# Hybrid decoder trunk on one NeuronCore: the triangular inverse of the recurrent stage on 16x16 blocks

## The chip, the cores and the metric

The kernel runs on one core of a Trainium2 chip. The metric is the device time of one execution in microseconds (us). A core has a matrix engine (TensorE, PE in the profile; its weight loads are listed apart as PEld), a vector engine (VectorE, DVE), a scalar engine (ScalarE, ACT), a general engine (GpSimd, POOL) and a queue that issues transfers (SyncE, SP). Each engine runs its own instructions in order and waits for others by semaphores. Products land in PSUM, which is read by DVE and ACT; the rest lives in SBUF.

## What is computed

One layer: RMSNorm, one input projection of 1024 x 4224 on 2048 tokens, and three branches side by side, each with a SiLU gate: differential attention (4 heads), a short gated convolution, and RWKV-7 time mixing (4 heads of size 64). The gated branches are joined, projected (1024 x 1024), added to the input and normalised. The RWKV branch is a recurrence over tokens:

```python
def step(state, inp):
    r_t, k_t, v_t, w_t, kk_t, a_t = inp
    sa = jnp.einsum('bhvk,bhk->bhv', state, kk_t)
    state = (state * w_t[:, :, None, :]
             - sa[..., None] * (kk_t * a_t)[:, :, None, :]
             + v_t[..., None] * k_t[:, :, None, :])
    y = jnp.einsum('bhvk,bhk->bhv', state, r_t)
    return state, y
```

Taken in chunks of 64 tokens, the feedback through `sa` inside a chunk becomes a unit triangular system of 64 x 64, and its inverse (Z in the code) turns the chunk into matrix products; only one 64 x 64 state per head goes from chunk to chunk.

## The kernel before

The tokens are worked in two halves of 1024. After a start stage (loads, norm, the projections that the recurrence needs) come four stages in this order: the recurrence of half 0 (called rwkv0 here), the attention of half 0, the recurrence of half 1 (rwkv1), the attention of half 1; a tail ends the output projection.

**Order on TensorE.** TensorE's order is that of the program text, written out by hand: each stage is a Python generator that yields hints (an amount of time), and `run` fills each hint with matmuls from one long list, the filler (`filler`): projections still to be made, and at the end the 16 tiles of the output projection (`out_tile`, L1184, 48 matmuls each). A hint f in a stage with factor `scale` draws matmuls of `T512` = 0.216 hint units each until f x scale is used up. SCALE is 0.6 for rwkv0 and 0.55 for rwkv1, 1.0 for attention. The other engines' orders are the compiler's. Output tile i is held back while i >= `allowed`; that is 8 until the first block of head 3 in the last attention is finished, and then 10, 12, 14, 16.

**The recurrent stage** (`rwkv`, L455) has 8 units per half, one for each 256 tokens and two heads. A unit passes through `early` (loads, decay, norms), `scores` (L549: scores G of the chunk, masked into N, BB and DE; part of N is written to memory as `ud` and read back as U in a layout with blocks spread over partitions), `inverse` (L632) and `late` (L660). The units are staggered: while `late` of unit n is emitted, after each of its yields one step of `early` and `scores` of unit n+2 follows, and then `inverse` of unit n+2.

**`inverse`** inverts the 32 x 32 diagonal blocks by substitution on DVE: 16 steps, each a multiplication (`tmpx`, L646) and a sum (`Xs`, L649) over 128 partitions. The result goes through memory (`zd`) into the diagonal blocks of Z.

**`late`** puts 64 x 64 inverses together: transposes of Z on TensorE (`xp`, L673), a copy to X, a product with N (`p4`, L680), a scaled copy into P1, a second product (`p5`, L685), an addition into Z (L688). All are 128 x 128 matmuls on block diagonal matrices. Then `wu` (Z times AB, L696), the products M and RW (`mr`, L717, L718) in two groups, and the short chain over the chunks (`chp`, `yp`, L738, L743) in which each step waits for a DVE copy of the state (`Ss`, L740).

PSUM has four pools here; `ps_w` (two buffers, `pw`) holds p4 and p5 together in one tile, and lw, la, ssp, bc2, vap, bvp, yp, vpp and bcp2; `ps_s` (three buffers, `pS`) holds G, tp, xp, wu, mr and the attention's scores.

**Broadcasts.** A factor per token is spread over 128 columns by a matmul with the identity: `bcp` (L538, L765), `obc` (L1066, 32 pairs in the attention stages) and `hbc` (`spread`, L251).

Of the kernel before, what the change touches and what calls it, by code (L numbers as in the profile page):

```python
# [24 lines left out]
NJ = 2  # L25
# [62 lines left out]
def _table(cols):  # L88
    t, o = {}, 0
    for n, w in cols:  # L90
# [7 lines left out]
                      ("eye", 32 * GW), ("hmean", 2), ("id64", 64), ("mB", 2)))  # L98
# [4 lines left out]
def host_consts():  # L103
    c, cr = np.zeros((P, NCON), np.float32), np.zeros((P, NCONR), np.float32)

    def put(n, a):
        d, (o, w) = (c, CON[n]) if n in CON else (cr, CONR[n])
        d[:, o:o + w] = a

    p = np.arange(P)  # L110
    t = np.arange(64)
    put("ident", np.eye(P))
    put("le", (p[:, None] % 64) <= t[None])
    put("lt", (p[:, None] % 64) < t[None])
# [5 lines left out]
    eye = np.eye(32).reshape(32, NG, GW).transpose(1, 0, 2).reshape(NG, 1, 32 * GW)  # L120
    put("eye", np.tile(eye.reshape(NG, 32 * GW), (NB, 1)))
# [24 lines left out]
def trunk(ctx, tc, a, o, phases="RTO"):  # L146
# [308 lines left out]
    def rwkv(half, pool):  # L455
# [21 lines left out]
        P1 = pool.tile([P, NQ, P], F32, name="P1")  # L477
        nc.gpsimd.memset(P1, 0.0)
        mB = C("mB")
# [7 lines left out]
        def early(s, n, g, ct):  # L487
# [61 lines left out]
        def scores(s):  # L549
# [17 lines left out]
            for jj in range(NJ // 2):  # L567
                for h in range(2):
                    G = pS("G")
                    for q in range(4):  # L570
                        j, e = jj * 2 + q // 2, q % 2
                        mm(G[:, q * P:(q + 1) * P], KB[h * 64:h * 64 + 64, j, 2 * e:2 * e + 2],  # L572
                           RA[h * 64:h * 64 + 64, :, j, 1 - e], start=True, stop=True)
                    Gv = G.rearrange("p (j e m t) -> p j e m t", j=2, e=2, m=2)
                    q0 = h * NJ + jj * 2
                    for e in range(2):
                        nr = slice(64 * e, 64 * e + 64)
                        sr = slice(64 - 64 * e, 128 - 64 * e)
                        lt = C("lt").unsqueeze(1).broadcast_to([P, 2, 64])
                        tt(N[sr, q0:q0 + 2, sr], Gv[sr, :, e, 1], lt[sr], ALU.mult)  # L580
# [5 lines left out]
            U = T("U", (P, 32, 32), bufs=2)  # L586
            ud = dr.tile([NB, 32, 32], F32, name="ud", bufs=2)
            for e in range(2):
                for b in range(2):
                    q0 = (e * 2 + b) * NQ  # L590
                    r0 = 64 - 64 * e + b * 32
                    dma(ud[q0:q0 + NQ].rearrange("q s t -> s q t"), N[r0:r0 + 32, :, r0:r0 + 32])
# [39 lines left out]
        def inverse(s):  # L632
            U, Z = s["U"], s["Z"]


            pr = T("U2", (P, 32, 16))
            Uf = U.rearrange("p s t -> p (s t)")
            tt(pr, U[:, :, 0:32:2], Uf[:, 1:1024:66].unsqueeze(1).broadcast_to([P, 32, 16]), ALU.mult)
            tt(U[:, :, 1:32:2], U[:, :, 1:32:2], pr, ALU.add)
            nc.gpsimd.memset(Uf[:, 0:1024:33], 1.0)  # L640
            Xs = T("Xs", (P, 32, GW))
            cpy(Xs, C("eye").rearrange("p (a b) -> p a b", a=32))
# [7 lines left out]
            Zs = T("Zs", (P, GW, 32))  # L650
            cpy(Zs, Xs.rearrange("p a b -> p b a"))
            zd = dr.tile([NB, 32, 32], F32, name="zd", bufs=2)
            dma(zd.rearrange("b (g c) i -> (b g) c i", c=GW), Zs)
            for e in range(2):
                for b in range(2):
                    q0 = (e * 2 + b) * NQ
                    r0 = 64 - 64 * e + b * 32
                    dma(Z[r0:r0 + 32, :, r0:r0 + 32], zd[q0:q0 + NQ].rearrange("q c i -> c q i"))

        def late(s):  # L660
            ct, gc, o0, N, Z = (s[n] for n in ("ct", "gc", "o0", "N", "Z"))
# [3 lines left out]
            Z2 = Z.rearrange("p q (b n) -> p q b n", b=2)  # L665
            Pb2 = P1.rearrange("p q (b n) -> p q b n", b=2)
# [3 lines left out]
            X = T("X", (P, NQ, 64))  # L670
            xp = pS("xp")
            for q in range(NQ):
                nc.tensor.transpose(xp[:, q * P:(q + 1) * P], Z[:, q], ident)  # L673
            yield LQ[0]
            cpy(X.rearrange("p q (b n) -> p (q b) n", b=2), xp.rearrange("p (q n) -> p q n", n=64)[:, :, 0:32])
            yield LQ[0]
            p45 = pw("p45")
            p4, p5 = p45[:, 0:NQ * 64], p45[:, NQ * 64:2 * NQ * 64]
            for q in range(NQ):
                mm(p4[:, q * 64:(q + 1) * 64], N[:, q], X[:, q], start=True, stop=True)  # L680
            yield LQ[0]
            act(Pb2[:, :, :, 0:32], p4.rearrange("p (q b n) -> p q b n", q=NQ, b=2), AF.Copy, scale=mB[:, 0:1])
            yield LQ[0]
            for q in range(NQ):
                mm(p5[:, q * 64:(q + 1) * 64], P1[:, q], Z2[:, q, :, 32:64], start=True, stop=True)  # L685
            yield LQ[0]
            Z64 = Z.rearrange("p q (b n) -> p (q b) n", b=2)
            stt(Z64[:, :, 32:64], p5.rearrange("p (q n) -> p q n", n=32), mB[:, 1:2], Z64[:, :, 32:64], ALU.mult,  # L688
                ALU.add)
# [13 lines left out]
            for r0 in (0, 64):  # L703
                nc.gpsimd.memset(Z[r0:r0 + 32, :, r0 + 32:r0 + 64], 0.0)
# [4 lines left out]
            RW = T("RW", (P, NJ, 2, 64))  # L709
            for e in range(2):  # L710
                sr = slice(64 - 64 * e, 128 - 64 * e)
                mr = pS("mr")[:, 0:2 * WR // 2]
                for h in range(2):
                    hs = slice(h * 64, h * 64 + 64)
                    for j in range(NJ):
                        q = h * NJ + j
                        mm(mr[hs, j * 64:j * 64 + 64], W[sr, q], KBm[sr, j * 2 + e, hs], start=True, stop=True)  # L717
                        mm(mr[hs, (NJ + j) * 64:(NJ + j) * 64 + 64], W[sr, q], DE[sr, q, e], start=True, stop=True)  # L718
                yield LQ[1]
                mr4 = mr.rearrange("p (m j n) -> p m j n", m=2, j=NJ)  # L720
# [43 lines left out]
            for j in range(NJ):  # L764
                mm(bcp[:, j * P:(j + 1) * P], rvb[:, 2 * j:2 * j + 2].rearrange("p a b -> p (a b)"), ident,  # L765
                   start=True, stop=True)
# [77 lines left out]
    def attention(half, nlam, bt, pool, after=None):  # L844
# [207 lines left out]
        def finish(h, pr, ob, sq, zs):  # L1052
# [12 lines left out]
            for j in range(2):  # L1065
                mm(bc[:, j * P:(j + 1) * P], rp[:, j:j + 1].broadcast_to([P, P]), ident, start=True, stop=True)  # L1066
# [318 lines left out]
```

## Time and profile before

| what | value |
|---|---|
| runs | median 1798.87 us of three (1794.3 to 1798.88) |
| the profiled execution | 1790.98 us, of which the span from first to last instruction is 1789.2 us |
| TensorE busy | 1615.6 us (90%) |
| DVE, POOL, ACT busy | 1229.6, 822.4, 733.4 us |
| mean granted TensorE clock | 0.955 of full speed |

Busy time counts overlapping matmuls once. Where the clock column says 0.50, TensorE had the lower of its two clocks (1.2 instead of 2.4 GHz). Waits are put down to the instruction that released them.

### The profile page before, as it was taken

What the parts mean: (1) busy time and instruction counts of PE and PEld (TensorE: products, weight loads), DVE (VectorE), ACT (ScalarE), POOL (GpSimd) and SP (SyncE); (2) the same over time, 40 slices, a digit from 0 to 9 for tenths busy, and PEclk for the clock granted to TensorE, in tenths of its full rate; (3) what the DMA queues carried; (4) which work ended last, traced back from release to release, by engine and by line L of the source; (5) the groups of instructions that cost most, each with busy time, mean ns of one, the idle gap of its engine ahead of it and who ended that gap; (6) DMA issues with size and microseconds to landing.
All of it is one profiled execution on the core that took longest, in us unless ns stands there. A gap on an engine that the chain in (4) does not pass through costs nothing.

```text
span 1789.2 us, 27288 instructions
## 1 busy us (share of the span) xinstructions
PE 1615.6 (90%) x9416; PEld 1300.2 (73%) x9416; DVE 1229.6 (69%) x2653; ACT 733.4 (41%) x1797; POOL 822.4 (46%) x794
## 2 busy tenths in 40 slices
PE   5899799999999878999799989998988979999998
PEld 4687576776788766778576767786777868877786
DVE  7633866677516788874766776518899898888842
ACT  5331111122115655552121222125656667767742
POOL 6433232333157886444132322275377375363243
PEclk9899898899899989999898999999999989999999
DMA  5343222222245634224222222253234243222223
GB/s 188 100 141 97 67 67 58 81 78 60 64 136 177 210 117 124 77 68 132 89 86 58 87 72 67 72 171 96 70 98 129 76 148 114 87 90 78 90 88 112
DMA packets 136586, 179.86 MB, mean 101 GB/s; under 512 B 34912, under 2 KB 83072, under 8 KB 136448
## 3 DMA queue, kind: packets, MB, share of 16 engines
q1 hardware_dynamic: 136448, 178.13, 31.9%
q8 instruction: 74, 1.21, 0.3%
q14 instruction: 64, 0.52, 0.1%
HBM read 131.92 MB, written 46.14 MB: 100 GB/s over the span
## 4 chain that ended last, share of the span: by engine, by line
PE 48%; DVE 33%; DMA 5%; issue 4%; ACT 4%; SPq 3%; POOL 3%; DVEq 0%; POOLq 0%; ACTq 0%
PE pj L343 23%; PE ops L1200 7%; DVE tmpx L646 5%; DVE P L992 4%; DVE Xs L649 3%; PE aT L1027 3%; DVE nm L949 3%; PE G L572 2%; SPq L594 2%; PE S L943 2%; PE S L944 2%; PE av L1020 2%; PE av L1018 1%; PE av L1019 1%; DVE x L242 1%
## 5 line engine op out<-in xcount | busy, mean ns | idle before, releaser
L343 PE MATMUL pj<-hh,wh 128*128 128x512 f32 x1008 | 420.7, 417 | 8.5 <-DVE raw L394 4.7
L343 PE MATMUL pj<-hl,wh 128*128 128x512 f32 x1008 | 420.5, 417 | 0.0
L343 PE MATMUL pj<-hh,wl 128*128 128x512 f32 x1008 | 419.9, 417 | 0.0
L952 ACT ACTIVATE P<-S,nm 128x512 f32<-128x512 f32 (+3 forms) x320 | 199.3, 624 | 151.1 <-DVE nm L949 134.9
L343 PEld LDWEIGHTS pj<-hh,wh 128*128 128x128 f32 x1008 | 195.7, 194 | 48.2 <-ACT hh L245 5.1
L329 POOL TENSOR_TENSOR wl<-wr,wh 128x1024 fp32r<-128x1024 f32 x85 | 209.2, 2461 | 46.0 <-ACT wh L324 41.0
L949 DVE TENSOR_REDUCE nm<-S 128x1 f32<-128x512 f32 (+3 forms) x320 | 191.5, 604 | 50.9 <-PE S L944 47.6
L343 PEld LDWEIGHTS pj<-hl,wh 128*128 128x128 f32 x1008 | 195.7, 194 | 40.0 <-issue 3.0
L343 PEld LDWEIGHTS pj<-hh,wl 128*128 128x128 f32 x1008 | 195.2, 194 | 40.3 <-issue 2.8
L992 DVE SCALAR_TENSOR_TENSOR P<-P,sc 128x512 f32<-128x512 f32 (+3 forms) x160 | 148.0, 950 | 6.8 <-ACT P L976 4.6
L326 POOL TENSOR_SCALAR wh<-wr 128x1024 fp32r<-128x1024 f32 x70 | 76.8, 1098 | 148.7 <-PE pj L343 142.2
L943 PE MATMUL S<-K,QH 128*128 128x512 f32 (+2 forms) x320 | 124.8, 390 | 22.2 <-ACT P L952 21.9
L646 DVE TENSOR_TENSOR tmpx<-U,Xs 128x16 f32<-128x16 f32 (+15 forms) x256 | 130.9, 511 | 6.6 <-POOL U L640 1.2
L1027 PE MATMUL aT<-con,P 128*128 128x128 f32 x576 | 91.6, 283 | 35.9 <-DVE aTl L1034 25.8
L944 PE MATMUL S<-K,QL 128*128 128x512 f32 (+2 forms) x320 | 119.0, 372 | 0.0
L1034 DVE TENSOR_TENSOR aTl<-aT,aTh 128x512 fp32r<-128x512 f32 x144 | 98.3, 684 | 26.5 <-ACT aTh L1033 24.9
L1027 PEld LDWEIGHTS aT<-con,P 128*128 128x128 f32 x576 | 70.0, 144 | 58.2 <-DVE aTl L1034 29.9
L1033 ACT CAST aTh<-aT 128x512 fp32r<-128x512 f32 x144 | 83.5, 583 | 51.3 <-PE aT L1027 50.7
L1200 PE MATMUL ops<-woh,wl 128*128 128x512 f32 x256 | 102.1, 399 | 0.0
L1200 PE MATMUL ops<-woh,wh 128*128 128x512 f32 x256 | 102.1, 399 | 0.0
L1200 PE MATMUL ops<-wol,wh 128*128 128x512 f32 x256 | 102.1, 399 | 0.0
L948 DVE TENSOR_TENSOR S<-S,bt 128x256 f32<-128x256 f32 (+1 forms) x152 | 57.2, 377 | 62.7 <-PE S L944 61.6
(337 smaller groups left out, 3345.4 us busy)
## 6 DMA issues: line engine op xcount, KB each, us to landing
wr<-in_wt_dram SPq DMA_DIRECT2D x85, 512.0 KB, 3.7
rawk<-pk SPq DMA_DIRECT2D x96, 128.0 KB, 2.8
U<-ud SPq DMA_DIRECT2D x128, 64.0 KB, 2.3
rawq<-pq SPq DMA_DIRECT2D x128, 64.0 KB, 2.3
wr<-mx SPq DMA_DIRECT2D x128, 64.0 KB, 2.0
oxt<-in_x_dram SPq DMA_DIRECT2D x32, 256.0 KB, 3.0
out_dram<-oxt SPq DMA_DIRECT2D x32, 256.0 KB, 2.1
prw<-s SPq DMA_DIRECT2D x28, 256.0 KB, 2.1
```

The lines of the kernel that those rows point to most:

```text
L329: nc.gpsimd.tensor_tensor(wl[:, ks], wr[:, ks], wh[:, ks].bitcast(F32), ALU.subtract)
L343: mm(ps, lhs[:, k], rhs[c][k], start=(n == 0), stop=(n == 3 * NK - 1))
L646: tt(tmp[:, :, :, 0:m], U[:, 0:m, i:i + 2].rearrange("p j r -> p r j").unsqueeze(2).broadcast_to([P, 2, GW, m]), Xs[:, 0:m].rearrange("p j ...
L943: mm(s[:, 0:sw], QH[:, m, off:off + P], K[:, m, 0:sw], start=True, stop=False)
L944: mm(s[:, 0:sw], QL[:, m, off:off + P], K[:, m, 0:sw], start=False, stop=True)
L949: nc.vector.tensor_reduce(nm[:, m, g:g + 1], s[:, 0:gw], AX.X, ALU.max, negate=True)
L952: act(p[:, 0:gw], s[:, 0:gw], AF.Exp, bias=nm[:, m, g:g + 1], accum_out=l[:, m, g:g + 1])
L992: stt(p1, p1, sc[:, 1, g:g + 1], p0, ALU.mult, ALU.add)
L1027: nc.tensor.transpose(t[:, d * 256 + qi * P:d * 256 + qi * P + P], x["A"][g][:, ko:ko + P], ident)
L1033: cpy(th, t)
L1034: tt(tl, t, th.bitcast(F32), ALU.subtract)
L1200: mm(ps, l[:, k], Ws[n][r][k], start=(c == 0), stop=(c == 3 * NK - 1))
```

## The change

Substitution works on 16 x 16 blocks: 8 steps in place of 16, with at most 128 in place of 256 products a partition in one. U, `ud` and `zd` shrink with it; the transfers of one unit become 8 writes of `ud` (4 before), 4 reads of U (8 before), 1 write of `zd`, and 8 reads into Z0 (4 before). 32 x 32 inverses are then made from 16 x 16 ones, and 64 x 64 from 32 x 32, each by two sets of small products on 32 x 32 tiles of the array; X comes from 32 x 32 transposes on DVE; N and Z hold only the 64 columns that are used. `late` has three more yields of `LQ[0]` = 0.9, and one yield of 2 x 0.5 where there were two of 0.5. `wu` is made of 64 x 64 tiles. The G products of both heads, and the `mr` products of both row halves, are issued alternately into two PSUM tiles. The broadcasts become transposes.

```diff
-NB = 4 * NQ
+BL = 16
+NB = 128 // BL * NQ
 NG = 128 // NB
-GW = 32 // NG
+GW = BL // NG
...
     def spread(rs, ps=None):
...
-            mm(ps[:, j * P:(j + 1) * P], rs[:, j:j + 1].broadcast_to([P, P]), ident, start=True, stop=True)
+            nc.tensor.transpose(ps[:, j * P:(j + 1) * P], rs[:, j:j + 1].broadcast_to([P, P]), ident)
...
-            for n, w in (("N", P), ("Z", P)):
+            for n, w in (("N", 64), ("Z", 64), ("Z0", 32)):
                 m[n] = pool.tile([P, NQ, w], F32, name=f"{n}{i}")
+            for n in ("Z", "Z0"):
                 nc.gpsimd.memset(m[n], 0.0)
...
             for j in range(NJ):
-                mm(bcp[:, j * P:(j + 1) * P], rnb[:, 2 * j:2 * j + 2].rearrange("p a b -> p (a b)"), ident,
-                   start=True, stop=True)
+                nc.tensor.transpose(bcp[:, j * P:(j + 1) * P], rnb[:, 2 * j:2 * j + 2].rearrange("p a b -> p (a b)"),
+                                    ident)
...
             for jj in range(NJ // 2):
+                Gs = [pS("G") for _ in range(2)]
+                for q in range(4):
+                    j, e = jj * 2 + q // 2, q % 2
+                    for h in range(2):
+                        mm(Gs[h][:, q * P:(q + 1) * P], KB[h * 64:h * 64 + 64, j, 2 * e:2 * e + 2],
+                           RA[h * 64:h * 64 + 64, :, j, 1 - e], start=True, stop=True)
                 for h in range(2):
-                    G = pS("G")
-                    for q in range(4):
-                        j, e = jj * 2 + q // 2, q % 2
-                        mm(G[:, q * P:(q + 1) * P], KB[h * 64:h * 64 + 64, j, 2 * e:2 * e + 2],
-                           RA[h * 64:h * 64 + 64, :, j, 1 - e], start=True, stop=True)
+                    G = Gs[h]
...
+            for r0 in (*range(64, 128, BL), *range(0, 64, BL)):
+                c0, q0 = r0 % 64, r0 // BL * NQ
+                dma(ud[q0:q0 + NQ].rearrange("q s t -> s q t"), N[r0:r0 + BL, :, c0:c0 + BL])
...
-            for i in range(0, 32, 2):
-                tmp = T("tmpx", (P, 2, GW, 32), bufs=1)
+            for i in range(0, BL, 2):
+                tmp = T("tmpx", (P, 2, GW, BL), bufs=1)
...
+            for r0 in range(0, P, BL):
+                c0, q0 = r0 % 32, r0 // BL * NQ
+                dma(Z0[r0:r0 + BL, :, c0:c0 + BL], zd[q0:q0 + NQ].rearrange("q c i -> c q i"))
...
+            X = T("X", (P, NQ, 32), bufs=2)
+            nc.vector.transpose(X, Z0)
             p45 = pw("p45")
+            p4, p5 = p45[:, 0:NQ * 16], p45[:, NQ * 16:NQ * 48]
+            blocks = [slice(r0, r0 + 32) for r0 in range(0, P, 32)]
             yield LQ[0]
             for q in range(NQ):
+                for rs in blocks:
+                    c0 = rs.start % 64
+                    mm(p4[rs, q * 16:(q + 1) * 16], N[rs, q, c0:c0 + 32], X[rs, q, 0:16], start=True, stop=True)
             yield LQ[0]
+            stt(P0[:, :, 0:16], p4.rearrange("p (q n) -> p q n", n=16), C("hi16"),
+                C("id16").unsqueeze(1).broadcast_to([P, NQ, 16]), ALU.mult, ALU.add)
+            yield LQ[0]
+            for q in range(NQ):
+                for rs in blocks:
+                    mm(p5[rs, q * 32:(q + 1) * 32], P0[rs, q], Z0[rs, q], start=True, stop=True)
+            yield LQ[0]
+            for i, rs in enumerate(blocks):
+                c0 = rs.start % 64
+                (nc.vector.tensor_copy if i % 2 == 0 else cpy)(Z[rs, :, c0:c0 + 32],
+                                                               p5[rs].rearrange("p (q n) -> p q n", n=32))
+
+            X = T("X", (P, NQ, 32), bufs=2)
+            for rs in blocks[0::2]:
+                nc.vector.transpose(X[rs], Z[rs, :, 0:32])
+            P1 = T("P1", (P, NQ, 32))
+            p45 = pw("p45")
+            p4, p5 = p45[:, 0:NQ * 32], p45[:, NQ * 32:2 * NQ * 32]
+            yield LQ[0]
+            for q in range(NQ):
+                for r0 in (0, 64):
+                    up, lo = slice(r0, r0 + 32), slice(r0 + 32, r0 + 64)
+                    mm(p4[lo, q * 32:(q + 1) * 32], N[up, q, 32:64], X[up, q], start=True, stop=True)
+            yield LQ[0]
+            cpy(P1[32:64], p4[32:64].rearrange("p (q n) -> p q n", n=32))
+            nc.vector.tensor_copy(P1[96:128], p4[96:128].rearrange("p (q n) -> p q n", n=32))
+            yield LQ[0]
+            for q in range(NQ):
+                for r0 in (0, 64):
+                    up, lo = slice(r0, r0 + 32), slice(r0 + 32, r0 + 64)
+                    mm(p5[up, q * 32:(q + 1) * 32], P1[lo, q], Z[lo, q, 32:64], start=True, stop=True)
+            yield LQ[0]
+            cpy(Z[0:32, :, 32:64], p5[0:32].rearrange("p (q n) -> p q n", n=32))
+            nc.vector.tensor_copy(Z[64:96, :, 32:64], p5[64:96].rearrange("p (q n) -> p q n", n=32))
             yield LQ[0]
...
-                    mm(wu[:, (h * NJ + j) * P:(h * NJ + j + 1) * P], Z[:, h * NJ + j], AB[:, j, h], start=True, stop=True)
+                    for hs in (slice(0, 64), slice(64, 128)):
+                        mm(wu[hs, (h * NJ + j) * P:(h * NJ + j + 1) * P], Z[hs, h * NJ + j], AB[hs, j, h], start=True,
+                           stop=True)
...
+            mrs = [pS("mr")[:, 0:2 * WR // 2] for _ in range(2)]
+            for j in range(NJ):
+                for what in range(2):
+                    for h in range(2):
+                        hs, q = slice(h * 64, h * 64 + 64), h * NJ + j
+                        for e in range(2):
+                            sr = slice(64 - 64 * e, 128 - 64 * e)
+                            mm(mrs[e][hs, (what * NJ + j) * 64:(what * NJ + j) * 64 + 64], W[sr, q],
+                               DE[sr, q, e] if what else KBm[sr, j * 2 + e, hs], start=True, stop=True)
+            yield 2 * LQ[1]
...
-                mm(bc[:, j * P:(j + 1) * P], rp[:, j:j + 1].broadcast_to([P, P]), ident, start=True, stop=True)
+                nc.tensor.transpose(bc[:, j * P:(j + 1) * P], rp[:, j:j + 1].broadcast_to([P, P]), ident)
```

## Rows read from the trace of the kernel before

**Rows 1.** The profile page: busy us, share of the span, instructions.
```profile
PE 1615.6 (90%) x9416; PEld 1300.2 (73%) x9416; DVE 1229.6 (69%) x2653; ACT 733.4 (41%) x1797; POOL 822.4 (46%) x794
```
**Rows 2.** Busy time by window: PE, PEld, DVE, ACT, POOL, clock, DMA share, GB/s.
```profile
160.00:511.00 351.00, 321.68 (x2215) 247.96 (x2214) 232.66 (x607) 67.22 (x170) 108.20 (x119) 0.93 0.22 66
...
822.00:1169.00 347.00, 316.98 (x2230) 243.95 (x2229) 224.09 (x604) 74.26 (x184) 105.70 (x123) 0.95 0.27 83
```
**Rows 3.** TensorE's waits in 160 to 511: total us, times, longest.
```profile
PE chp L738 <- DVE Ss L740: 9.8, 6, 3.8
PE xp L673 <- DMA Z<-zd: 8.6, 1, 8.6
```
**Rows 4.** TensorE's waits in 822 to 1169.
```profile
PE xp L673 <- DMA Z<-zd: 7.1, 2, 5.4
PE chp L738 <- DVE Ss L740: 4.5, 4, 2.7
```
**Rows 5.** Timeline of all engines, 440.5 to 446.2: start, duration, instruction.
```profile
441.22 0.66 DVE L646 TENSOR_TENSOR tmpx<-U,Xs 128x256 f32<-128x256 f32 x1
...
442.32 2.49 POOL L329 TENSOR_TENSOR wl<-wr,wh 128x1024 fp32r<-128x1024 f32 x1
...
442.52 2.44 DVE L558 TENSOR_TENSOR RA<-in_r,PL 128x128 f32<-128x128 f32 x1
...
445.56 0.48 PE L738 MATMUL chp<-Ss,M 64*64 64x64 f32 x4 [2.43 <-DVE Ss L740]
```
**Rows 6.** Busy time by window, 450 to 455, columns as in rows 2.
```profile
450.00:455.00 5.00, 5.00 (x26) 3.48 (x24) 2.29 (x9) 0.56 (x2) 0.00 (x0) 0.50 0.04 7
```
**Rows 7.** DVE's groups by line: busy us, mean ns, idle before.
```profile
L646 DVE TENSOR_TENSOR tmpx<-U,Xs 128x16 f32<-128x16 f32 (+15 forms) x256 | 130.9, 511 | 6.6 <-POOL U L640 1.2
L649 DVE TENSOR_REDUCE Xs<-tmpx 128x8 f32<-128x16 f32 (+15 forms) x256 | 74.8, 292 | 6.0
```
**Rows 8.** TensorE's timeline, one unit: blocks of matmuls and what starts next.
```profile
405.12 1.16 PE L572 MATMUL G<-RA,KB 64*128 64x128 f32 x8
406.20 0.50 PE L343 MATMUL pj<-hh,wl 128*128 128x512 f32 x1
...
415.14 0.68 PE L618 MATMUL bvp<-VU,BB 64*64 64x64 f32 x16
415.75 0.50 PE L343 MATMUL pj<-hh,wl 128*128 128x512 f32 x1
...
418.16 0.61 PE L765 MATMUL bcp<-con,sqy 128*128 128x128 f32 x4
418.52 0.48 PE L343 MATMUL pj<-hl,wh 128*128 128x512 f32 x1
...
426.22 1.00 PE L680 MATMUL p<-X,N 128*128 128x64 f32 x8
427.03 0.48 PE L343 MATMUL pj<-hh,wl 128*128 128x512 f32 x1
...
437.55 0.32 PE L717 MATMUL mr<-KBm,W 64*64 64x64 f32 x2
...
438.44 0.50 PE L343 MATMUL pj<-hh,wh 128*128 128x512 f32 x1
```
**Rows 9.** Timeline, ACT's groups, and waits of weight loads around lw.
```profile
423.34 0.70 PE L496 MATMUL lw<-in_thw,wup 64*128 64x256 f32 x2
...
L501 ACT ACTIVATE e<-lw,der 128x256 f32<-128x256 f32 x16 | 7.6, 476 | 32.4 <-PE la L498 23.3 <-PE lw L496 9.2
...
PEld p L680 <- ACT e L501: 3.5, 9, 0.4
```
**Rows 10.** Chain in order of time; output matmuls until 1643; a window before it.
```profile
89.24 65.76 PE pj L343 x281
...
L1200 PE MATMUL ops<-woh,wh x120: 387/393/628, 1444.7 to 1642.8; 128*128 128x512 f32 x120
...
1600.00:1643.00 43.00, 41.30 (x230) 34.95 (x229) 34.97 (x75) 30.71 (x76) 19.18 (x21) 1.00 0.23 73
```

More of the change, by code (lines that the diff above doesn't have):

```diff
@@ L119, in host_consts @@
     put("cmat", np.eye(P) - same / 64.0)
-    eye = np.eye(32).reshape(32, NG, GW).transpose(1, 0, 2).reshape(NG, 1, 32 * GW)
-    put("eye", np.tile(eye.reshape(NG, 32 * GW), (NB, 1)))
+    eye = np.eye(BL).reshape(BL, NG, GW).transpose(1, 0, 2).reshape(NG, BL * GW)
+    put("eye", np.tile(eye, (NB, 1)))
+    put("hi16", (p[:, None] % 32) >= 16)
+    put("id16", (p[:, None] % 32) == np.arange(16)[None])
+    put("id16b", (p[:, None] % 32) == 16 + np.arange(16)[None])
     put("hmean", ((p[:, None] // 64) == np.arange(2)[None]) / 64.0)
@@ L472, in rwkv @@
             m = {}
-            for n, w in (("N", P), ("Z", P)):
+            for n, w in (("N", 64), ("Z", 64), ("Z0", 32)):
                 m[n] = pool.tile([P, NQ, w], F32, name=f"{n}{i}")
+            for n in ("Z", "Z0"):
                 nc.gpsimd.memset(m[n], 0.0)
             mats.append(m)
-        P1 = pool.tile([P, NQ, P], F32, name="P1")
-        nc.gpsimd.memset(P1, 0.0)
-        mB = C("mB")
+        P0 = pool.tile([P, NQ, 32], F32, name="P0")
+        nc.gpsimd.tensor_copy(P0[:, :, 16:32], C("id16b").unsqueeze(1).broadcast_to([P, NQ, 16]))
         def T(n, shape=(P, WR), bufs=1):
@@ L585, in scores @@
                        C("le").unsqueeze(1).broadcast_to([P, 4, 64]), ALU.mult)
[L586 to L592, printed above, removed]
+            U = T("U", (P, BL, BL), bufs=2)
+            ud = dr.tile([NB, BL, BL], F32, name="ud", bufs=2)
+            for r0 in (*range(64, 128, BL), *range(0, 64, BL)):
+                c0, q0 = r0 % 64, r0 // BL * NQ
+                dma(ud[q0:q0 + NQ].rearrange("q s t -> s q t"), N[r0:r0 + BL, :, c0:c0 + BL])
             for cg in range(NG):
@@ L632, in inverse @@
         def inverse(s):
[L633 to L636 removed]
+            U, Z0 = s["U"], s["Z0"]
+            h2 = BL // 2
+            pr = T("U2", (P, BL, h2))
             Uf = U.rearrange("p s t -> p (s t)")
[L638 to L642, printed above, removed]
[L643 to L644 removed]
+            tt(pr, U[:, :, 0:BL:2], Uf[:, 1:BL * BL:2 * BL + 2].unsqueeze(1).broadcast_to([P, BL, h2]), ALU.mult)
+            tt(U[:, :, 1:BL:2], U[:, :, 1:BL:2], pr, ALU.add)
+            nc.gpsimd.memset(Uf[:, 0:BL * BL:BL + 1], 1.0)
+            Xs = T("Xs", (P, BL, GW))
+            cpy(Xs, C("eye").rearrange("p (a b) -> p a b", a=BL))
+            for i in range(0, BL, 2):
+                tmp = T("tmpx", (P, 2, GW, BL), bufs=1)
                 m = i + 2
@@ L649, in inverse @@
                 nc.vector.tensor_reduce(Xs[:, i:i + 2], tmp[:, :, :, 0:m], AX.X, ALU.add)
-            Zs = T("Zs", (P, GW, 32))
+            Zs = T("Zs", (P, GW, BL))
             cpy(Zs, Xs.rearrange("p a b -> p b a"))
-            zd = dr.tile([NB, 32, 32], F32, name="zd", bufs=2)
+            zd = dr.tile([NB, BL, BL], F32, name="zd", bufs=2)
             dma(zd.rearrange("b (g c) i -> (b g) c i", c=GW), Zs)
[L654 to L658, printed above, removed]
+            for r0 in range(0, P, BL):
+                c0, q0 = r0 % 32, r0 // BL * NQ
+                dma(Z0[r0:r0 + BL, :, c0:c0 + BL], zd[q0:q0 + NQ].rearrange("q c i -> c q i"))
         def late(s):
-            ct, gc, o0, N, Z = (s[n] for n in ("ct", "gc", "o0", "N", "Z"))
+            ct, gc, o0, N, Z, Z0 = (s[n] for n in ("ct", "gc", "o0", "N", "Z", "Z0"))
             RA, DE, VU, VU4, AB, KBm = (s[n] for n in ("RA", "DE", "VU", "VU4", "AB", "KBm"))
@@ L669, in late @@
                                     s["PC"].unsqueeze(2).broadcast_to([P, NC, 64]), ALU.mult)
[L670 to L676, printed above, removed]
-            p45 = pw("p45")
-            p4, p5 = p45[:, 0:NQ * 64], p45[:, NQ * 64:2 * NQ * 64]
@@ L679, in late @@
[L679 to L682, printed above, removed]
+            X = T("X", (P, NQ, 32), bufs=2)
+            nc.vector.transpose(X, Z0)
+            p45 = pw("p45")
+            p4, p5 = p45[:, 0:NQ * 16], p45[:, NQ * 16:NQ * 48]
+            blocks = [slice(r0, r0 + 32) for r0 in range(0, P, 32)]
@@ L709, in late @@
             RW = T("RW", (P, NJ, 2, 64))
-            for e in range(2):
[L711 to L720, printed above, removed]
+            mrs = [pS("mr")[:, 0:2 * WR // 2] for _ in range(2)]
[8 more added lines that the diff above has]
+            yield 2 * LQ[1]
+            for e in range(2):
+                mr4 = mrs[e].rearrange("p (m j n) -> p m j n", m=2, j=NJ)
                 tt(M[:, :, e], mr4[:, 0], dP4[:, :, e], ALU.add)
@@ L764, in late @@
             for j in range(NJ):
-                mm(bcp[:, j * P:(j + 1) * P], rvb[:, 2 * j:2 * j + 2].rearrange("p a b -> p (a b)"), ident,
-                   start=True, stop=True)
+                nc.tensor.transpose(bcp[:, j * P:(j + 1) * P], rvb[:, 2 * j:2 * j + 2].rearrange("p a b -> p (a b)"),
+                                    ident)
             yield LQ[1]
```

14 lines of the change are left out of this document (2 added, 12 removed).

## The prediction

> **What bounds the kernel now.** I read the page first: TensorE is busy 90% of the span [rows 1], so what a change wins must come out of TensorE's idle time, its clock or its own work, and what it adds there it loses. Then the windows by stage, since the change lives in two stages. In rwkv0 (160 to 511) TensorE is busy 321.7 of 351 us, in rwkv1 (822 to 1169) 317.0 of 347 [rows 2]: 29.3 + 30.0 = 59 us idle. The clock column is the second loss: 0.93 and 0.95, so 0.07 x 351 + 0.05 x 347 = 42 us of full-speed work is missing. DVE is busy only two thirds of these stages, but that is an average.
>
> Then the waits of TensorE in these stages. Two kinds stand out: the first `late` of each half waits for Z from the inverse, 8.6 + 7.1 us, and the chain over the chunks waits for DVE's copy of the state, 9.8 + 4.5 us in ten places [rows 3, 4]. The timeline shows why the copy is late [rows 5]: at 441 DVE still runs the last substitution steps of another unit (0.66 us for one multiplication) between the short operations that `late` needs, one of those is stretched to 2.44 us while POOL runs a 2.49 us subtraction, and the chunk product at 445.56 has waited 2.43 us. The wait has an echo: at 450 to 455 TensorE is busy all the time, at clock 0.50, the lower of its two levels [rows 6], and it had idled just before. So a stall of 2 us costs more than 2 us. Shorter substitution can take both away.
>
> **The substitution.** One unit spends (130.9 + 74.8) / 16 = 12.9 us of DVE in the 16 steps [rows 7]. The 8 steps that stay have the shapes of the smaller half (up to 128 products a partition); at 0.7 of the mean durations that is 8 x 0.7 x (0.51 + 0.29) = 4.5 us, an estimate. Work that comes to DVE: three transposes, one small fused operation and four copies out of PSUM. No row shows a DVE transpose; it lies between nothing and, as an estimate, the 0.3 us of a reduction in the steps removed [rows 7], which is what I take, for eight operations 2.4 us less one that goes. DVE is relieved by 12.9 - 4.5 - 2 = about 6 us a unit, and the inverse of a unit is ready about 8 us earlier, so it no longer runs beside the chain over the chunks.
>
> Term 1, waits. The wait for Z at the start of a half goes (8 us earlier against 8.6 and 7.1): -14. Of the 14.3 us for the state copies I take 10; of the other 29 us, spread over G, wu, bc and others, 6, since POOL's long operations stay. Sum -30. Bounds: -15 (only Z) and -59 (all).
>
> Term 2, clock. I let it go in the same share as the waits: 42 x 30 / 59 = -21. Bounds -10 and -42.
>
> The transfers are not on the path: 17 of them become 21 per unit, fewer bytes each, and after the first unit of a half Z is wanted a whole unit (351 / 8 = 44 us) after it was started. If that cover is gone, it is the Z wait of the first unit that grows.
>
> **TensorE's own small products.** A block's price is the time from its start to the next filler matmul [rows 8]. Removed per unit: p4, p5 and wu, three blocks of 8 records at 427.03 - 426.22 = 0.81 each, and the xp transposes, 4 records, which I price like the 4 of bcp, 0.36: 2.8 us. (A matmul in this precision leaves two records, a transpose one.) Added: 32 + 32 records on 32 x 32 tiles for the first level, 16 + 16 for the second, 16 for wu. No row shows 32 x 32 tiles. The two nearest are bvp, 16 records that change between two corners of the array, 0.61 us or 0.038 each, and mr, 16 records that mostly stay in one corner, 438.44 - 437.55 = 0.89 or 0.056 each. The new products walk over two or four tiles on the diagonal, which is bvp's pattern: 96 x 0.038 = 3.65, plus wu with twice the columns, 0.95, plus about 0.1 to enter one more block: 4.7, so +1.9 us a unit. G (two blocks of 1.08 us) and mr now alternate between row halves with the same columns, which no row shows side by side: between no gain and half (-1.0 for G, 2 x 0.89 to 32 x 0.038, -0.6, for mr). I take three quarters: -1.2. The two broadcasts save half of 0.36 each: -0.36. Sum about +0.3 us a unit, term 3 = +4 with 16 units. Bounds: -4 (full gain on G and mr) and +64 (small tiles at mr's pace: 96 x 0.056 + 16 x 0.11 = 7.1, so +4.3 a unit, no gain on G and mr, and -0.36).
>
> A rule of the Trainium skill speaks against this step: TensorEngine Tiling (Array Packing), section Tiling Modes, says that changing the tiling mode, not just the tile, drains TensorE. bvp's block, which enters and leaves such a mode, costs 0.61 us in all [rows 8], which leaves no room for two drains as long as a matmul. By the page the sum below would come to +11 in place of -29 (rival c).
>
> **A wait that comes in.** p4 now precedes lw and la, and the tile that holds p4 and p5 keeps one of the two buffers of `ps_w` until Z is copied out. lw takes the other, and la, issued right behind lw, must wait until ACT has read lw. That such reuse makes TensorE wait is seen today (p4 waits for the same ACT operation nine times, 0.4 us at most, with filler in between) [rows 9]. Now there is none in between: 0.70 for lw and 0.48 for ACT, less the third of lw's time that its records take anyway: 0.95 us. Behind la stand the filler and then the stage's own products. It happens in the units in which `early` of another unit runs beside `late`, 6 per half: term 4 = 12 x 0.95 = +11. Bounds 0 and +15.
>
> **Filler drawn earlier.** Three more yields of 0.9 in `late` draw 2.7 x 0.6 x 8 / 0.216 = 60 matmuls more in rwkv0, and 55 in rwkv1. One takes 65.76 / 281 = 0.234 us [rows 10], so 27 us move out of later stages into these two. They come back only if the later stage is bound by TensorE. Until 1643, when head 3's first block ends, 358 output matmuls have run (three groups of 120, 119, 119) [rows 10]; tile 8 is not let in before, which is 384. With 115 more the list is held at 384: 89 matmuls find no place before 1643 and leave gaps instead, and 26 shorten the tail by 6 us. In the 43 us before 1643 DVE is busy 35.0 [rows 10], so that stretch shrinks by at most 8. Term 5 = 27 - 6 - 8 = +13. Bounds 0 and +27.
>
> **Broadcasts in attention.** 32 blocks of obc with four records become two: 32 x 0.18 = -6 (term 6), as TensorE is the busiest engine there. Bounds 0 and -6.
>
> **The sum**: -30 - 21 + 4 + 11 + 13 - 6 = -29, from the profiled execution's 1790.98 to 1762. Its own time lies 7.9 us under the median of the runs, so the median after should be 1770. A change under 0.3% (5 us) is about what cannot be told from none.
>
> **Rivals.** (a) The waits are the whole story: if every listed stall goes and the clock stays up, terms 1 and 2 are -59 and -42, the sum -79, 1720 us. For it: the stalls sit where DVE is full. Against it: POOL's long operations still stretch DVE's.
> (b) The gain is handed back: DVE's stretched operations [rows 5] keep the state copies late, only the Z waits go (-15, clock -10), and the filler comes back badly (+20): -15 - 10 + 4 + 11 + 20 - 6 = +4, 1803 us.
> (c) Drain: the array runs empty on entering and on leaving each of the five blocks p4, p5, p4, p5 and wu. A pair of mr records lasts 0.32 us from start to end [rows 8], which I take as the time to run empty: 5 x 2 x 0.32 x 16 = 51 in place of the 11 or so that I have for entries. Sum -29 + 40 = +11, 1810 us. The rule named above is of this kind; the trace speaks against it, by bvp.
> (d) Slower: the small products run at mr's pace, 0.056 a record. Then term 3 is +64 and the sum +31, 1830 us. It decides from 0.038 + 29 / (16 x 112) = 0.054 us a record on; it is the same number of records that would have to show 0.054.
>
> **Chances.** Forecast (1735 to 1792) 0.62; (a) 0.15; (b) 0.09, of it 0.03 faster, 0.04 same, 0.02 slower; (c) 0.05, of it 0.01 same, 0.04 slower; (d) 0.09. Faster 0.62 + 0.15 + 0.03 = 0.80, same 0.05, slower 0.15. The range 1715 to 1808 takes in (b), most of (a) and half of (c), and leaves out (d) and the far ends.
>
> **What would show it.** Right: tmpx and Xs fall to 128 each and under 5 us a unit; the waits of chp for Ss and of the first product of `late` for the transferred block fall below 10 us over both halves; the clock of the two stages reaches 0.97; la shows a wait of about 1 us for the ACT operation on lw; the last 43 us before head 3's first block ends show fewer output matmuls. Wrong: records of p4 and p5 0.05 us apart or more; DVE busy to the brim beside the chain as before; the stages as long as before although the waits are gone, which would be the filler alone.

## The result, and the profile after

The change made the kernel slower: 1813.62 us (median of four runs, 1812.19 to 1815.42) against 1797.39 us for the kernel before, a ratio of 1.0093 with a 95% interval of [1.0074, 1.0112]. Forecast were 1770 us, in a range of 1715 to 1808. The profiled execution took 1812.19 us, with a span of 1810.4.

The busy line of the page after the change:

```profile
PE 1586.0 (88%) x10616; PEld 1247.1 (69%) x10616; DVE 1134.5 (63%) x2509; ACT 734.5 (41%) x1829; POOL 800.7 (44%) x762
```

Against [rows 1], TensorE is busy 29.6 us less and the span is 21.2 us longer: idle time grew by 51 us. The windows by stage say where. In each row: stretch, its length, busy time of PE, PEld, DVE, ACT and POOL with their instructions, clock, DMA share, GB/s. After the change, the five stretches are rwkv0 (from 160 us on), attention of half 0, rwkv1, attention of half 1, tail:

```profile
160.00:543.00 383.00, 347.54 (x3056) 256.13 (x3057) 192.19 (x542) 73.48 (x196) 128.50 (x131) 0.93 0.24 69
543.00:846.00 303.00, 251.44 (x1279) 210.39 (x1278) 227.70 (x478) 159.53 (x432) 181.04 (x181) 0.91 0.39 118
846.00:1216.00 370.00, 339.60 (x3049) 250.54 (x3048) 179.56 (x535) 79.40 (x205) 120.84 (x131) 0.95 0.28 83
1216.00:1767.00 551.00, 479.25 (x2549) 397.48 (x2548) 445.24 (x857) 347.12 (x846) 281.51 (x253) 0.96 0.31 95
1767.00:1810.40 43.40, 36.16 (x155) 28.78 (x154) 9.43 (x18) 10.87 (x22) 15.28 (x13) 0.95 0.32 109
```

The same cuts before the change:

```profile
160.00:543.00 383.00, 353.68 (x2359) 273.98 (x2358) 234.68 (x611) 71.37 (x177) 135.37 (x146) 0.93 0.26 77
543.00:823.00 280.00, 248.77 (x1315) 207.98 (x1314) 218.69 (x475) 157.93 (x427) 177.71 (x179) 0.96 0.39 124
823.00:1199.00 376.00, 345.98 (x2359) 267.46 (x2359) 225.11 (x608) 78.41 (x191) 130.53 (x149) 0.95 0.30 91
1199.00:1739.00 540.00, 492.36 (x2663) 412.04 (x2662) 454.52 (x856) 348.43 (x848) 284.30 (x250) 0.97 0.32 98
1739.00:1789.20 50.20, 42.96 (x186) 34.13 (x184) 13.26 (x21) 12.92 (x26) 19.48 (x17) 0.98 0.35 113
```

The stages that were changed are as long as before (+0, -6). The time was lost where no instruction of consequence changed: +23 in the attention of half 0, +11 in that of half 1, -7 in the tail.

The waits of TensorE, in rwkv0 and then in rwkv1, after the change (total us, times, longest):

```profile
PE la L501 <- ACT e L504: 12.9, 6, 4.1
PE chp L765 <- DVE Ss L767: 11.6, 8, 1.9
PE G L575 <- DVE KB L563: 2.7, 2, 2.3
...
PE chp L765 <- DVE Ss L767: 13.1, 8, 2.6
PE G L575 <- DVE KB L563: 6.2, 2, 3.1
PE la L501 <- ACT e L504: 3.8, 6, 1.0
```

Against [rows 3, 4]: the wait for the block that comes back from memory (8.6 + 7.1) is gone, the wait for the state copy grew from 14.3 to 24.7 us, and la brought 16.7.

Substitution and the new transposes, DVE's groups after the change (busy, mean ns | idle before):

```profile
L650 DVE TENSOR_TENSOR tmpx<-U,Xs 128x16 f32<-128x16 f32 (+7 forms) x128 | 52.4, 410 | 6.2 <-POOL U L644 3.3
L653 DVE TENSOR_REDUCE Xs<-tmpx 128x8 f32<-128x16 f32 (+7 forms) x128 | 28.7, 224 | 3.1
L696 DVE STREAM_TRANSPOSE X<-Z 32x128 f32<-32x128 f32 x32 | 9.6, 301 | 0.9
L672 DVE STREAM_TRANSPOSE X<-Z 128x128 f32<-128x128 f32 x16 | 5.0, 311 | 19.8 <-DMA Z<-zd 14.7 <-DMA mx<-th 3.0 <-DMA pza<-th 1.6
```

The steps now cost (52.4 + 28.7) / 16 = 5.1 us a unit where [rows 7] had 12.9. The transposes cost 0.30 and 0.31 us each.

The new products among the filler, TensorE's timeline after the change (start, duration):

```profile
389.62 0.45 PE L687 MATMUL p<-Z,P 32*32 32x32 f32 x32
390.01 0.50 PE L345 MATMUL pj<-hh,wl 128*128 128x512 f32 x1
...
393.90 0.44 PE L704 MATMUL p<-X,N 32*32 32x32 f32 x16
394.27 0.50 PE L345 MATMUL pj<-hl,wh 128*128 128x512 f32 x1
...
406.63 1.16 PE L575 MATMUL G<-RA,KB 64*128 64x128 f32 x16
407.72 0.50 PE L345 MATMUL pj<-hl,wh 128*128 128x512 f32 x1
...
423.85 0.44 PE L680 MATMUL p<-X,N 32*32 32x16 f32 x32
424.21 0.50 PE L345 MATMUL pj<-hh,wh 128*128 128x512 f32 x1
```

Priced from a block's start to the next filler matmul, as in [rows 8], 32 records on 32 x 32 tiles take 0.36 to 0.39 us, and 16 records 0.37. G of two heads together takes 1.09, as much as one head did.

### The profile page after: what moved, and what is told of

It reads as the page before. It is cut to its first block, busy times and chain, and to the rows that moved or that the text cites. A ratio compares the mean times of both kernels' runs of the same rounds, so it can differ in the third digit from the quotient of the medians.

```text
span 1810.4 us, 29652 instructions
## 1 busy us (share of the span) xinstructions
PE 1586.0 (88%) x10616; PEld 1247.1 (69%) x10616; DVE 1134.5 (63%) x2509; ACT 734.5 (41%) x1829; POOL 800.7 (44%) x762
## 4 chain that ended last, share of the span: by engine, by line
PE 54%; DVE 26%; DMA 5%; issue 5%; ACT 4%; SPq 3%; POOL 3%; DVEq 0%; POOLq 0%; ACTq 0%
PE pj L345 27%; PE ops L1227 7%; DVE P L1019 4%; DVE nm L976 3%; PE aT L1054 3%; DVE tmpx L650 2%; PE S L970 2%; PE S L971 2%; PE av L1047 1%; DVE aTl L1061 1%; PE av L1045 1%; PE av L1046 1%; DVE x L244 1%; PE G L575 1%; ACT P L979 1%
## 5 line engine op out<-in xcount | busy, mean ns | idle before, releaser
L345 PE MATMUL pj<-hh,wh 128*128 128x512 f32 x1008 | 426.1, 423 | 10.2 <-ACT ccs L255 6.5
L345 PE MATMUL pj<-hh,wl 128*128 128x512 f32 x1008 | 425.2, 422 | 1.0 <-POOL wl L331 1.0
L345 PEld LDWEIGHTS pj<-hh,wl 128*128 128x128 f32 x1008 | 198.9, 197 | 44.0 <-issue 4.1
L1019 DVE SCALAR_TENSOR_TENSOR P<-P,sc 128x512 f32<-128x512 f32 (+3 forms) x160 | 141.5, 916 | 10.2 <-ACT P L1003 8.2
L1054 PE MATMUL aT<-con,P 128*128 128x128 f32 x576 | 95.4, 292 | 48.3 <-DVE aTl L1061 23.4
L970 PEld LDWEIGHTS S<-K,QH 128*128 128x128 f32 x320 | 63.4, 198 | 57.9 <-ACT P L979 42.0
L1003 ACT ACTIVATE P<-P,sc 128x512 f32<-128x512 f32 (+3 forms) x144 | 87.4, 660 | 37.3 <-DVE sc L998 36.7
```

The costliest lines, as they stand in the source:

```text
L345: mm(ps, lhs[:, k], rhs[c][k], start=(n == 0), stop=(n == 3 * NK - 1))
L970: mm(s[:, 0:sw], QH[:, m, off:off + P], K[:, m, 0:sw], start=True, stop=False)
L1003: act(pt[0, g][:, 0:gw], pt[0, g][:, 0:gw], AF.Copy, scale=sc[:, 0, g:g + 1])
L1019: stt(p1, p1, sc[:, 1, g:g + 1], p0, ALU.mult, ALU.add)
L1054: nc.tensor.transpose(t[:, d * 256 + qi * P:d * 256 + qi * P + P], x["A"][g][:, ko:ko + P], ident)
```

## Experiments

One theory stood at the start. F: the time is lost because the three added yields draw filler out of the later stages, whose work is then badly placed. Its rivals: the wait of la (L), the new order of G (B), the broadcasts as transposes (O), the small products themselves. Ratios are to the kernel before, with 95% intervals.

**The filler alone, both ways.** In the changed kernel `late` yields as much in all as before; in the kernel before it yields as much as after.

```diff
 (changed kernel, ten places in late)
-            yield LQ[0]
+            yield LQ[0] * 0.7
 (kernel before, seven places in late)
-            yield LQ[0]
+            yield LQ[0] * 10 / 7
```

> The changed kernel with the ten hints of 0.9 in `late` cut to 0.63, so that the recurrent stages draw as much filler as before the change. Theory F (the 115 matmuls drawn early set the loss: the norm loads and the scaling of half 1 now fall into other places of the attention): the recurrent stages get 14 and 13 us shorter, the attention of half 0 falls from 303 to about 281 us, that of half 1 from 550 to about 540, the tail grows by 6: 1813 - 52 = about 1761 us, ratio to the kernel before 0.98. Rival O (the attention is slower for another reason, the transposed broadcasts or another order on DVE and ACT): the attention of half 0 stays near 300 us, and only the rearrangement shows: 1795 to 1813 us.

> The kernel before with the seven hints of 0.9 in `late` raised to 0.9 x 10 / 7, so that it draws as much filler in the recurrent stages as the changed kernel; nothing else differs. Theory F: recurrent stages longer by 14 and 13 us, attention of half 0 longer by some 20, that of half 1 by some 9, tail shorter by 6: 1797 + 50 = about 1847 us, at the least 1820. Rival O: what is drawn early is saved later, 1797 to 1808 us.

Measured: 1759.99 us, 0.9821 [0.9771, 0.9872], and 1854.63 us, 1.034 [1.0291, 1.0389]. The same amount of filler costs 1.0093 - 0.9821 = 0.0272 or 49 us in the new code and 61 us in the old. Windows of the first of the two, the same five stages:

```profile
160.00:524.00 364.00, 332.98 (x2990) 244.59 (x2989) 188.82 (x539) 70.97 (x192) 125.13 (x129) 0.94 0.23 69
524.00:797.00 273.00, 243.38 (x1278) 201.85 (x1277) 220.68 (x475) 157.39 (x427) 176.97 (x179) 0.96 0.41 128
797.00:1167.00 370.00, 334.74 (x2999) 245.71 (x2998) 185.70 (x536) 79.16 (x207) 120.00 (x133) 0.93 0.27 83
1167.00:1707.00 540.00, 489.40 (x2630) 409.51 (x2629) 456.74 (x856) 347.77 (x848) 280.62 (x250) 0.97 0.32 98
1707.00:1757.30 50.30, 43.04 (x186) 34.43 (x184) 13.56 (x21) 12.81 (x26) 19.88 (x17) 0.95 0.34 113
```

Both attentions are as short as before the change or shorter (273 and 540). So the added filler is the cause, in size too; how it makes the later stages longer is asked below.

**la in another pool of PSUM.**

```diff
-            la = pw("la")[:, 0:WR]
+            la = pS("la")[:, 0:WR]
```

> The changed kernel with la in a buffer of the pool of three, so that la need not wait for ACT to read lw; TensorE's order and the filler stay. If the 16.7 us that la waits are on the path: 1813 - 17 = 1797 us, a few more with the clock. Rival: the same ACT operation holds the next product (ssp, or p5 behind DVE) just as long: 1808 to 1815 us.

Measured: 1795.97 us, 1.0008 [0.998, 1.0035]. Rival L is real but smaller than F: 0.0085, 15 us. How one such wait gets to 4 us shows on ACT and then on TensorE, in the timeline after the change (in brackets the idle time and its releaser):

```profile
429.22 0.30 ACT L655 COPY Zs<-Xs 128x64 f32<-128x64 f32 x1 [4.68 <-DVE Xs L653]
429.56 0.24 ACT L646 COPY Xs<-conr 128x64 f32<-128x64 f32 x1
429.71 0.47 ACT L504 ACTIVATE e<-lw,der 128x256 f32<-128x256 f32 x1
...
430.23 0.79 PE L501 MATMUL la<-in_thw,wup 64*128 64x256 f32 x1 [4.09 <-ACT e L504]
```

The reading of lw stands in ACT's order behind a copy that waits for the end of a substitution.

**The broadcasts alone**, in the kernel before; so also for `bcp` and `hbc`:

```diff
-                mm(bc[:, j * P:(j + 1) * P], rp[:, j:j + 1].broadcast_to([P, P]), ident, start=True, stop=True)
+                nc.tensor.transpose(bc[:, j * P:(j + 1) * P], rp[:, j:j + 1].broadcast_to([P, P]), ident)
```

> The kernel before with only the broadcasts turned into transposes (bcp, obc and hbc). Forecast term 6 and the broadcast part of term 3: 32 x 0.18 + 16 x 0.36 = 11.5 us less on TensorE, 1797 - 8 = about 1789 us. Rival O: the transposes are what slows the attention stages: 1797 + 10 to 20 us.

Measured: 1794.85 us, 1.0005 [0.9981, 1.0029]. They neither harm nor help.

**Which place in the attention costs.** Two moves in the changed kernel: the constants that start the attention on a smaller draw of filler, and the norm of the second half's inputs 60 matmuls later in the list.

```diff
-START = (26.477, 25.0)
+START = (26.477 - 12.96, 25.0 - 11.88)
```
```diff
-        rs = [stats(c) for c in range(2)]
+        rs = []
+ (in the loop over att_steps(0, 3))
+            if n == 60:
+                rs.extend(stats(c) for c in range(2))
```

> The changed kernel as it is, all ten hints of 0.9 kept, but the hints that open the two attention stages cut by 12.96 and 11.88, so that the first score of each attention comes at the same place of the filler list as before the change. Theory F (place of the attention in the filler list): attention of half 0 at 273 to 281 us, of half 1 at 540, all in all as with the cut hints, 1760 us. Rival P (the wider spacing inside `late` costs, or the narrower one gains): attention better but the recurrent stages not, 1775 to 1800 us.

> The changed kernel with one step of the filler moved: the loads and squares for the norm of half 1 come 60 filler matmuls later, which is where they stood against the attention before the change; the scaling that uses them stays where the change put it. If those loads are what blocks ACT and the transfers at the start of the attention of half 0: that stage gets about 10 us shorter, 1803 us. Rival: the scaling is the dear part and now waits for its loads as well: 1810 to 1820 us.

Measured: 1788.04 us, 0.9974 [0.9948, 1.0], and 1818.32 us, 1.0135 [1.0084, 1.0185]. The first gives a part back and is no clean test: the attention of half 0 took 291 us, with TensorE waiting 9.2 us for POOL's copy of Q and 6.3 for ACT at S. The second changed nothing there: 302 us. The loss only went from the first block to the second: the first three blocks of that attention end 46, 68 and 97 us after its start in the changed kernel, and here 37, 65 and 90 (before the change 34, 48 and 70).

So the scaling of those inputs (`make_h1`), which follows in the list, was moved too: with the norm (60, first chunk 60, second chunk 20 later), and without it.

```diff
-        yield from seq(att_steps(0, 3), lambda c: make_h1(c, rs[c]))
...
+            if n == 60:    # 0 in the second kernel
+                rs.extend(stats(c) for c in range(2))
+            if n == 96 + 60:
+                make_h1(0, rs[0])
+            if n == 192 + 20:
+                make_h1(1, rs[1])
```

> The changed kernel with the norm of the second half and the scaling of its inputs moved back in the filler list by the number of matmuls that the change moved them ahead: norm loads and squares 60 matmuls later, scaling of the first chunk 60 later, of the second 20 later (it is needed there). The ends of the first four blocks of the attention of half 0 are at 16, 34, 48 and 70 us after its start before the change, and at 16, 46, 68 and 97 after it. Theory P (the place of this work in the attention makes it long): blocks end near 36, 50 and 74 again, the attention of half 0 takes 285 to 290 us in place of 303, and the time is 1795 to 1800 us. Rival Q (it is the attention's own projections, shifted in the list, with their splits on GpSimd, or the smaller amount of filler left): the attention stays at 300 to 303, the time at 1813.

> The changed kernel with the scaling alone moved back (60 and 20 matmuls later), the norm loads and squares where the change put them. With the earlier run that moved the norm alone this makes four cases. Theory P: the second block stays at 30 us, since the squares still fall into it, the third and fourth come down towards 14 and 22: the attention of half 0 about 293 us, the time about 1803. If only both together matter it is as long as after the change (303, 1813). Rival Q: 303, 1813.

(The 16 in the text on record is no block's end; the blocks are the three named above.) Measured: 1807.54 us, 1.0083 [1.0058, 1.0109], and 1807.39 us, 1.0074 [1.0045, 1.0102]. With both moved, the attention of half 0 took 289 us, blocks ending at 34, 56 and 78:

```profile
542.00:831.00 289.00, 242.18 (x1277) 202.55 (x1276) 232.32 (x477) 158.79 (x432) 178.99 (x180) 0.94 0.40 123
```

With the scaling alone it took 300. In the profiles, then, the place of norm and scaling together is 14 of the 23 us; each alone mends little. What is left enters in the fifth block (counted from one broadcast `obc`, which closes a block, to the next): it takes 28 us in the changed kernel and with both moved, where it took 11 before the change. The scaling of the second chunk, moved by only 20 matmuls, still lies in it, and the filler matmul that needs it waits, in the kernel with both moved from 648 to 678 us:

```profile
PE pj L345 <- DVE hl L248: 12.2, 1, 12.2
```

The whole time does not show the 14 us: the intervals overlap with that of the changed kernel, the attention of half 1 was 4 us longer in that profile, and the profiled execution (1799.51 us) was the fastest of eight.

**Repairs put together.** The edits of the first and the third kernel above (`LQ[0] * 0.7` and la in `ps_s`); then the copy of the state on ACT as well:

```diff
-                nc.vector.tensor_copy(sst[ct] if c == NC - 1 else Ss[:, c + 1], chp[:, c * 64:(c + 1) * 64])
+                cpy(sst[ct] if c == NC - 1 else Ss[:, c + 1], chp[:, c * 64:(c + 1) * 64])
```

> Both repairs together: hints cut to 0.63 and la in the other pool. In the first, la still waited 10.4 us: 1760 - 10 to 17 = about 1748 us. Rival: with the shorter hints the wait moves on to the next product that ACT or DVE must release: 1757 to 1762 us.

> As the kernel with both repairs, and the copies of the state between chunks go to ACT, away from the masks and scalings that stand before them on DVE. The waits for them are some 22 us in the two stages: if they are on the path, 1748 - 15 to 22 = about 1730 us. Rival: ACT's copy takes as long behind its own queue, or the chunk products wait for other things: within 4 us of the kernel with both repairs.

Measured: 1745.05 us, 0.9731 [0.9682, 0.978], and 1706.23 us, 0.9518 [0.9466, 0.9569], which beats both kernels, and the 1730 us expected of it by 24 us. Windows of its two recurrent stages:

```profile
160.00:501.00 341.00, 319.18 (x2997) 234.05 (x2997) 175.08 (x509) 77.78 (x225) 127.78 (x130) 0.98 0.25 75
...
780.00:1115.00 335.00, 316.33 (x2995) 232.69 (x2994) 171.87 (x503) 85.20 (x239) 119.98 (x131) 0.97 0.30 90
```

The clock reaches 0.98 and 0.97, where the kernel with both repairs has 0.95 and 0.94, and no wait for the state copy is among the longest: in rwkv0 the first two are

```profile
PE p L712 <- DVE P L707: 3.2, 1, 3.2
PE G L575 <- DVE KB L563: 2.7, 2, 2.3
```

The same edit in the kernel before:

> The kernel before with the state copies on ACT and nothing else. If DVE's order was what kept the copies late there too: the 14.3 us of waits go and half of the 42 us that the clock costs in the two stages: 1797 - 14 to 35 = about 1772 us. Rival: beside the 32 x 32 substitution the next wait (G for its scaled operands) takes over: 1790 to 1797 us.

Measured: 1774.29 us, 0.9891 [0.986, 0.9922]. It is worth 0.0213 in the repaired kernel and 0.0109 in the old one, whose waits for Z (7.0 and 7.6) remain; the clock of the two stages rises there too, to 0.97 and 0.97.

**The order of G.** Why is the state copy late although DVE has less to do? In the kernel with filler and la repaired, G was put back to one head after the other:

```diff
-                Gs = [pS("G") for _ in range(2)]
-                for q in range(4):
...
-                    for h in range(2):
-                        mm(Gs[h][:, q * P:(q + 1) * P], ...
+                for h in range(2):
+                    G = pS("G")
+                    for q in range(4):
+                        j, e = jj * 2 + q // 2, q % 2
+                        mm(G[:, q * P:(q + 1) * P], ...
```

> The kernel with both repairs (1745 us), with the G products again head by head in two blocks. Theory B (since the G of both heads comes in one block, ten masks follow on DVE in one stretch and the state copy stands behind them): the waits for the state copies fall from some 22 to under 12 us over both stages, but TensorE pays 1.07 us more a unit, 17 in all: 1750 to 1758 us. Rival: the copies are late because POOL stretches DVE's operations: the waits stay above 18 us and the time goes to 1762 us or more.

Measured: 1747.67 us, 0.9737 [0.9718, 0.9756], no change in time. But the waits for the state copy fell from 10.1 + 10.5 to 4.0 + 2.3. B is right on the wait; what it saves is paid again by the second block of G: in the two stages TensorE is busy 670.7 us in place of 654.4. The clock stays where it was, at 0.95 in both stages (0.95 and 0.94 without this edit). DVE's timeline in the changed kernel shows the wait being made:

```profile
409.39 0.29 DVE L585 TENSOR_TENSOR N<-G,conr 64x128 f32<-64x128 f32 x1
409.71 0.28 DVE L586 TENSOR_TENSOR BB<-G,conr 64x128 f32<-64x128 f32 x1
409.92 0.27 DVE L585 TENSOR_TENSOR N<-G,conr 64x128 f32<-64x128 f32 x1
410.23 0.29 DVE L586 TENSOR_TENSOR BB<-G,conr 64x128 f32<-64x128 f32 x1
410.55 0.23 DVE L767 COPY Ss<-chp 128x64 f32<-128x64 f32 x1
```

The state's product ended at 408.5; five masks of the first head and then these four of the second stand ahead of the copy, and the next state product waited 1.34 us at 410.83.

**Is the old filler the right amount for the best kernel?**
```diff
-            yield LQ[0] * 0.7
+            yield LQ[0] * 0.85    # 0.5 in the second kernel
```

> The fastest kernel so far (1706 us) with the ten hints at 0.85 of 0.9 in place of 0.7, which draws about 30 filler matmuls more in each recurrent stage, half of what the change drew. Theory F, if the loss grows with the shift: half of the 50 us, 1725 to 1735 us. Rival (a step that is met or not met): either 1706 to 1713 or 1750 us and more.

> The same with the hints at 0.5 of 0.9: some 39 filler matmuls fewer in each recurrent stage. Theory F says only that the place in the list matters; the attention of half 0 then meets the scaling of half 1 later than before the change. If the place before was near the best one: 1715 to 1730 us. If less filler is simply better: 1690 to 1700 us.

Measured: 1741.63 us, 0.9707 [0.9691, 0.9723], and 1736.99 us, 0.9686 [0.967, 0.9702]. Both expectations were too mild: either way costs over 30 us. The attention of half 0 takes 298 and 290 us in place of 279; the tail is 44 and 68 in place of 50.

## Why the prediction was wrong

**The step that failed is term 5, the filler drawn earlier.** The prediction had the mechanism and the number of matmuls (115, 27 us into the two stages, 6 out of the tail, and a list held at 384), and then wrote that the 27 us "come back only if the later stage is bound by TensorE" and that the last stretch "shrinks by at most 8": +13, and +27 at the most. It took for granted that no attention gets longer. Measured is +49 (the changed kernel with and without it) and +61 (the old one with it). In the new code that is, by stage, +19, +30, 0, +11 and -7. The attention of half 0, which the prediction left at nothing, is the largest part: work that hangs on the list, not only the matmuls, came 60 matmuls earlier in it. Of the 23 us that it is longer than before, 14 go with the place of norm and scaling, in the profile, and the rest enters in the fifth block, with the second scaling in it. Why the whole time did not follow the 14 stays open.

In the attention of half 1 the hold at 384 came as foretold, and dearer. In the changed kernel the 384th output matmul starts at 1628.81, and the next 41 us later; then come the same 41 us as a window, and the last 41 us before head 3's first block ends in the kernel before:

```profile
1628.81 0.39 PE L1227 MATMUL ops<-woh,wl 128*128 128x512 f32 x1
...
1669.85 0.80 PE L1227 MATMUL ops<-woh,wh 128*128 128x512 f32 x1 [2.89 <-ACT wh L1207]
...
1629.00:1670.00 41.00, 28.63 (x158) 22.25 (x157) 33.41 (x79) 30.07 (x77) 14.24 (x20) 0.87 0.14 41
...
1602.00:1643.00 41.00, 39.30 (x217) 33.17 (x216) 33.58 (x73) 29.50 (x74) 17.55 (x19) 1.00 0.24 76
```

TensorE stands idle for 12 of these 41 us, where it idled for 2. The stretch was to shrink for want of matmuls, but that block ends 445 us after the start of its stage, before the change 444. The stage gets longer behind it: 8 us pass from there (1661.95) to the next output matmul, and the rest then takes 96 us as before. With the old filler there is no such gap in the changed kernel, and with more filler the kernel before has one of 40 us, again after 384. The gap is not all that can lengthen this stage: with the smaller draw at the start it took 555 us without one.

**Without that step the sum was nearly right, through errors that cancel.** The other terms make -42; measured is 0.9821, -32 us with an interval of -41 to -23. As an estimate from what was measured term by term below (waits for Z -16, state copies +10, small products -48, la +15, the rest nothing) the sum is -39. One by one:

- *Substitution*: 5.1 us a unit for 4.5 forecast, and DVE relieved by (42.5 + 45.5) / 16 = 5.5 us a unit for 6. Right.
- *Term 1, waits* (-30): the Z waits went, 15.7 us for 14. The state copies were to give 10 and cost 10: the prediction saw the substitution in front of the copies and missed that G of both heads in one block puts the masks of both there. With the old order of G in the repaired kernel they are 6.3 us, 8 less than before the change, which fits the 10 forecast for the shorter substitution. Wrong in half.
- *Term 2, clock* (-21): 0.93 and 0.95 as in [rows 2], so nothing. It was tied to the waits, and these did not fall. The tie itself is not shown: with the state on ACT the waits went and the clock rose, in both kernels, but with the old order of G the same waits fell by 14 us and the clock stayed at 0.95.
- *Term 3, small products* (+4): mis-sized. The five blocks cost 0.39 + 0.36 + 0.37 + 0.37 + 1.02 (wu) = 2.5 us a unit where 2.8 were removed; G saves 1.07, mr 1.16 (its 32 records take 0.62 together), the two broadcasts 0.46. That is -3.0 a unit, -48 in all, an estimate from block prices, outside the bounds on the good side (the bound of -4 is -1 when its own terms are added). TensorE's busy time in the two stages fell by 32 us at the old filler, and by 50 between the two kernels with the state on ACT, whose clocks are nearly alike (la differs there too). The price per record was taken from bvp (0.038); measured is 0.39 / 32 = 0.012.
- *Term 4, la* (+11): the mechanism as foretold, 12 places; 16.7 us of waits and 15 us of time, since some of ACT's readings stand behind a copy that waits.
- *Term 6, obc* (-6): not seen, 1.0005.

**The rivals.** The time fell near (c), 1810, but not by its cause: the Trainium skill, TensorEngine Tiling (Array Packing), section Tiling Modes, says that a change of mode drains TensorE, and this trace shows no room for a costly drain, as a whole block of 32 records with its entry and exit takes 0.36 us. The same section says that tiles work independently, so that different tiles load weights and multiply in parallel; with that the trace agrees (G's halves side by side: 1.09 us for twice the records), and it was the sentence to bound term 3 by. (d) needed 0.054 a record and saw 0.012. (b) named the state copies, rightly, and the filler at +20, in direction right and in size not.

## What to carry to other kernels

Where one hand-ordered list of filler feeds several stages, a change in a stage's hints moves everything behind it in the list, including the loads, norms and scalings that hang on it: cost the later stages at their new places, keep the sum of the hints when a stage is cut into more steps, and where the list can be held, count what is left for the time of the hold. Where a chain over chunks waits for a copy, look at what stands ahead of the copy in its engine's order after the change, and try the copy on another engine: here it was worth 38 us in the repaired kernel. When a forecast comes out as a sum of terms of both signs, test the largest assumption of "nothing changes there" first.

## What the runs showed of the hardware that was not expected

Records on 32 x 32 tiles that go round the diagonal cost 0.011 to 0.012 us each, entry and exit of their block included (32 in 0.36 to 0.39 us), and 16 on 64-row halves, alternating, take 1.09 us where 8 took 1.08. A block of 16 small records that goes over two tiles costs the same 0.37 as one of 32 that goes over four: it is eight records a tile in both. A DVE transpose in blocks takes the same time over 32 partitions (301 ns) as over 128 (311 ns).
